# One block of hybrid attention and gated delta rule: the second group's load of the 32x32 inverses goes behind the spill stores on SP's queue

## The chip, the cores and the metric

The kernel runs on one core of one Trainium2 chip. The core has five engines that run side by side: TensorE (PE: matrix products, results in PSUM banks), VectorE (DVE), ScalarE (ACT), GpSimd (POOL) and SyncE (SP). In this kernel all transfers between SBUF and device memory are issued by SP, one after the other, in an order fixed at compile time: an issue that has to wait holds up every issue behind it. The metric is the time of one execution on the device, in microseconds; smaller is better.

## The reference

One transformer block on 1024 tokens of width 1024, in float32. What is computed:

- `h = rmsnorm(x) * (1 + sc1) + sh1`, and `proj = h @ w_in`, which is split into q, k, v of the attention (8 heads of 64) and q, k, v, z, b, a of the gated delta rule (8 heads of 64). `sh1, sc1, g1, sh2, sc2, g2` come from `silu(c) @ w_ada + b_ada`.
- Dilated attention over three window and dilation pairs with a bias by distance, the three results mixed by their softmax denominators.
- The gated delta rule: a causal convolution of width 4 and SiLU on q, k, v; then chunks of tokens, in which a unit lower triangular system is solved,

```python
a_mat = jnp.where(strict, jnp.einsum('nbhcd,nbhed->nbhce', k_beta, kc) * decay, 0.0)
sol = lax.linalg.triangular_solve(a_mat + jnp.eye(CHUNK), rhs, left_side=True, lower=True, unit_diagonal=True)
```

  and a state that is carried from chunk to chunk.
- `x = x + g1 * (concat(attention, delta) @ w_out)`, then a gated feed-forward `(silu(h @ w_gate) * (h @ w_up)) @ w_down`, and a last rmsnorm.

## The kernel before

Every float32 product is done as three products of halves (`hi*hi + lo*hi + hi*lo`): ACT makes the rounded half (`wh`), POOL or DVE the rest (`wl`). Tokens lie in 8 blocks of 128 (`TB`).

**The two groups of delta heads.** `delta(g)` handles four heads at a time: group 0 first, then group 1 (called the second group here). The delta rule is done in chunks of 128, and a chunk's triangular matrix is inverted in two stages in `delta_inverse(g)`. First all 128 diagonal 32x32 blocks of the group (4 heads, 8 chunks, 4 blocks) are inverted at once, one block per partition, by 31 steps of two DVE instructions each (L889, L893). The result `tt` has one inverse in each partition. It is stored to device memory (`tn_d<-tt`, L896) and loaded back as `tn` (L898) with the rows of the blocks on the partitions: 128 partitions of 32 runs of 32 numbers, that is 4096 runs of 128 bytes. Second, four `head`s join the 32x32 inverses to 64x64 and 128x128 by small matmuls (`lv` L921, L937, L941, `lw` L951, `lx` L959), with DVE transposes of `tn` into `U` (L926) and ACT copies of it (L928, L929) beside them. Then `delta_scan(g)` carries the state over the chunks.

**Work counted off ahead.** The projections that are not needed yet are a stream of big matmuls, `others()`, in the order z0, kd, qd, vd, z1 and then, for each pair of attention heads, `va` (L613, eight slices of 24 matmuls, one per token block), the key projection `a4` and the query projection `a0` (L590, two halves of 24 matmuls each). `ahead(us)` takes so many microseconds of that stream by a nominal price (0.64 for three matmuls of 512 columns, 0.32 for three of 256); `until` takes from it until a product is done. `hold(what, us)` does both, and is called once in each `delta_inverse`, at step 0 of the heads: `LEVELS = ("qd", 4), ("z1", 46)`. For the second group z1 is done long before, and by the prices the 46 us are the rest of `va0`, all of `a4_0` and `a0_0`, and six of the eight slices of `va1`. After it, `front` is the last matmul that was counted off and `evicted` the last copy out of PSUM; the heads' first matmuls are put behind `front` on PE, their copies behind `evicted` on ACT. So the heads of the second group begin on PE after the sixth slice of `va1`.

**How a product leaves.** A product is summed up in one of two PSUM banks (`gbank`). ACT copies it, in pieces of 128x256, into a tile with the tag `ev`, of which there are four, and SP stores the tile. `spill` does this for the halves of `kd`, `qd`, `vd`, `a4` and `a0` (copy L1100, store L1101, two of each to a half), `va_evac` for the slices of `va` (copy L1091, store L1092). A tile comes free when its store has landed; a bank when its copies are done. ACT works in order too, so a copy that waits for a tile holds up the copies behind it.

**What sets the order.** The program is traced in Python, and a planner gives each engine a fixed order: it plays the program through with its own estimates of times, and when an engine is free in that play, it takes of the ready instructions the one that was traced first. `urgent()` moves a block 6000 places forward (weight loads L229, the copies out of PSUM; not the stores). `tc.issue_after(x)` adds an edge: what the block traces on the engine of `x` comes behind `x` in that engine's order, with no wait for `x` to end. So the place of a load in SP's queue follows from where it is traced, from when the planner thinks that it is ready, and from such edges.

Of the kernel before, what the change touches and what calls it, by code (L numbers as in the profile page):

```python
# [18 lines left out]
P = 128  # L19
# [4 lines left out]
HALF = 512  # L24
# [7 lines left out]
LEVELS = ("qd", 4), ("z1", 46)  # L32
# [50 lines left out]
def build(tc, I, out):  # L83
    nc = tc.nc
# [20 lines left out]
    def urgent():  # L105
        return tc.high_priority(offset=6000)
# [420 lines left out]
    def scratch(name, n, shape):  # L527
        return [dr.tile(shape, F32, name=f"{name}{i}_d") for i in range(n)]

    class _:  # L530
# [6 lines left out]
        tn = scratch("tn", 2, [P, 1024])  # L537
# [22 lines left out]
    last, taken = [None], [None]  # L560
# [3 lines left out]
    def ahead(us):  # L564

        some = us > 0
        while us > 0:
            w = next(fill[0], None)
            if w is None:
                break  # L570
            us -= w
            used[0] += w
        return some and last[0] is not None
# [296 lines left out]
    def delta_inverse(g, st):  # L870
# [14 lines left out]
        for j in range(31):  # L885
# [9 lines left out]
            )  # L895
        nc.sync.dma_start(_.tn[g], ttf)  # L896
        tn = pr.tile([P, 32, 32], F32, name=f"tn{g}", tag="dt", bufs=2)
        nc.sync.dma_start(  # L898
            tn,
            bass.AP(tensor=_.tn[g].tensor, offset=_.tn[g][0:1, :].offset, ap=[[32, P], [4096, 32], [1, 32]]),  # L900
        )
        st["U"] = []

        def head(hl_):
# [59 lines left out]
        for step in range(3 * SKEW + 8):  # L964
            for h in heads:
                next(h, None)
            if step % SKEW == 0 and step // SKEW < 4:
                if step == 0:
                    hold(*LEVELS[g])
                    front, evicted, quiet[0] = last[0].ins, taken[0], True  # L970
                heads.append(head(step // SKEW))
                with tc.issue_after(front):
                    next(heads[-1])
# [113 lines left out]
    def va_evac(c):  # L1087
# [4 lines left out]
            nc.sync.dma_start(_.va[c][:, :, tb].rearrange("i p d -> p i d"), t.rearrange("p (i d) -> p i d", i=2))  # L1092
        return f

    def spill(name, dst):
        def f(hf, ps):
            for i in range(2):
                t = pv.tile([P, 256], F32, name=f"sp_{name}_{hf}_{i}", tag="ev", bufs=4)
                with urgent():
                    taken[0] = nc.scalar.copy(t, ps[:, 256 * i : 256 * i + 256])  # L1100
                nc.sync.dma_start(dst[:, HALF * hf + 256 * i : HALF * hf + 256 * i + 256], t)  # L1101
        return f

    def va_end(c):
# [46 lines left out]
    def others():  # L1151
        def group1(which):
            for i, (kind, col) in enumerate((("kd", KD), ("qd", QD), ("vd", VD))):
                if kind in which:
                    for q in range(2):
                        yield from proj_d(col + 2 + q, f"{kind}{2 + q}", spill(f"{kind}{q}", _.pj[2 * i + q]))
                    done.add(kind)

        yield from proj_t(I["wz0"], 256, "z0", z_evac(0))
        yield from group1(("kd", "qd", "vd"))  # L1160
        yield from proj_t(I["wz1"], 256, "z1", z_evac(1))
        done.add("z1")
        for hp in range(4):
            if hp < 2:
                yield from proj_t(I["wva"][hp], 256, f"va{hp}", va_end(hp))
                done.add(f"va{hp}")
            for col, kk in ((KA, 4), (QA, 0)):
                yield from proj_d(col + hp, f"a{kk}_{hp}", spill(f"a{kk}_{hp}", _.qk[kk + hp]))
            done.add(hp)
# [11 lines left out]
    quiet = [False]  # L1181
    fill[0] = mixed()

    def hold(what, us):

        until(lambda: what in done)
        ahead(us)

    def until(ready):
        while not ready():  # L1190
            used[0] += next(fill[0])
# [23 lines left out]
    def delta(g, made=(None, None)):  # L1215
        st = {}
        kt = []
        for j in range(4):
            kind, q = ("k", j) if j < 2 else ("q", j - 2)
            hp = 2 * g + q  # L1220
            t = pd.tile([P, T], F32, name=f"{kind}d{hp}", tag=f"{kind}d", bufs=2)
            (kd if kind == "k" else qd)[hp] = t
            if g == 0:
                conv((4 if kind == "k" else 0) + hp, xps[j], t)
                kt.append(delta_turn(g, kind, q, t, norms=norms[0], keep=kind == "k"))
                if j == 1:
                    nc.scalar.activation(norms[0]["lr"], norms[0]["rk"], AF.Ln, bias=eps1)
            else:
                nc.sync.dma_start(t, _.cv[j])
                if kind == "k":  # L1230
                    kt.append(delta_turn(g, kind, q, t, keep=True))
        delta_prep(g, st, norms[g], kt[0:2], made[0] or delta_rows(g))
        if g == 1:
            until(lambda: "vd" in done)
        delta_v(g, st, [lambda q=q: vxp[q] if g == 0 else fetch(4 + q, f"v{2 + q}") for q in range(2)], made[1])
        delta_inverse(g, st)
        until(lambda: ("qd", "z1")[g] in done)
        delta_scan(g, st)
        return None if g else delta_early()
# [289 lines left out]
    for hf in range(2):  # L1529
# [4 lines left out]
        for d in range(KT):  # L1534
            slabs = [(wsplit(I["wo"][d, 0], 512, f"wo{d}_0_{hf}"), 0)]
            t = x2[d, hf]
# [206 lines left out]
    for k in range(4):  # L1743
# [3 lines left out]
        t = px.tile([P, HALF], F32, name=f"t2_{k}", tag="m", bufs=5)  # L1747
# [260 lines left out]
```

## Time and profile before

| | |
|---|---|
| time, median of 3 runs | 1400.84 us (1399.38 to 1406.18) |
| the profiled execution's own time | 1404.82 us |
| its span, first to last instruction | 1403.1 us |
| PE busy, share of the span | 1350.7 us, 96% |
| DVE, ACT, POOL busy | 63%, 47%, 20% |
| mean granted TensorE clock | 0.988 |

The profile has rows of groups of instructions (line, engine, operation, output <- input, count, durations), waits (who stood idle until what), a timeline, and busy times in stretches of the span. `SPq` is the issue of a transfer: its time is that of issuing, not of moving the data. In the timeline, neighbouring instructions of one kind are merged into one row with a count. PEclk is the clock that TensorE was granted, 1.00 at full speed. All positions are microseconds from the start of the span.

### The profile page before, as it was taken

How to read it: one execution, taken by the hardware profiler on the slowest of the kernel's cores; microseconds unless marked ns; L12 is line 12 of the kernel's file. 1: busy time of each engine (PE TensorE's matmuls, PEld its weight loads, DVE VectorE, ACT ScalarE, POOL GpSimd, SP SyncE). 2: the span in 40 equal slices, each digit the busy share in tenths (PEclk: the TensorE clock that was granted, in tenths of full speed). 3: DMA queues.
4: the chain of work that ended last, by engine and by line, in shares of the span. 5: the costliest groups of instructions: out<-in, count | busy, mean ns of one | idle time of the engine just before them, and what ended most of it. 6: DMA issues, size and time to landing. Idle time of an engine off the chain costs nothing.

```text
span 1403.1 us, 24422 instructions
## 1 busy us (share of the span) xinstructions
PE 1350.7 (96%) x8984; PEld 1114.8 (79%) x8984; DVE 877.0 (63%) x1677; ACT 661.7 (47%) x1287; POOL 284.1 (20%) x267
## 2 busy tenths in 40 slices
PE   8999999999989899999999999999999999999998
PEld 4778887888888777778877878888888888888876
DVE  3687484666825433666228987667575776474497
ACT  4497424356224255766147743333333333444455
POOL 2346412344213244443162000000000000000000
PEclk9999899999999999999999999999999999999999
DMA  8665565475452355441584345444453665765575
GB/s 309 224 194 167 138 219 175 135 250 173 129 144 68 104 164 173 141 123 54 180 262 151 121 165 173 165 160 166 139 196 113 210 210 187 257 225 191 191 263 195
DMA packets 169872, 245.68 MB, mean 175 GB/s; under 512 B 32566, under 2 KB 73831, under 8 KB 169752
## 3 DMA queue, kind: packets, MB, share of 16 engines
q1 hardware_dynamic: 169752, 244.12, 53.4%
q8 instruction: 71, 1.16, 0.3%
q14 instruction: 49, 0.40, 0.1%
HBM read 181.30 MB, written 67.48 MB: 177 GB/s over the span
## 4 chain that ended last, share of the span: by engine, by line
PE 54%; DVE 5%; DMA 3%; issue 2%; ACT 2%; POOL 1%; SPq 0%; DVEq 0%; ACTq 0%; POOLq 0%
PE wua L1602 9%; PE wga L1602 8%; PE X L1802 6%; PE wo L590 5%; PE wgc L1602 4%; PE wuc L1602 4%; PE g_a L590 3%; PE Z L1802 3%; PE wgb L1602 2%; PE y L1359 2%; PE Y L1802 2%; PE wub L1602 2%; PE tr L1338 2%; PE S L1314 1%; PE S L1315 1%
## 5 line engine op out<-in xcount | busy, mean ns | idle before, releaser
L1592 DVE TENSOR_TENSOR wl_db<-wr_db,wh_db 128x512 fp32r<-128x512 f32 x77 | 52.9, 690 | 67.0 <-ACT wh_db L1591 66.8
L1591 ACT CAST wh_db<-wr_db 128x512 fp32r<-128x512 f32 x77 | 47.5, 622 | 85.3 <-PE X L1802 39.4
L1318 DVE CUSTOM_DVE_ANT_0 X<-S,ng 128x512 f32<-128x512 f32 (+3 forms) x64 | 36.9, 587 | 60.0 <-PE S L1315 40.0
L1325 POOL TENSOR_SCALAR X<-X,sc 128x128 f32<-128x128 f32 (+7 forms) x64 | 49.0, 769 | 77.1 <-DVE sc L1324 71.6
L1802 PE MATMUL X<-wl_db,wh_da 128*128 128x512 f32 x160 | 62.4, 390 | 0.3 <-DVE wl_db L1592 0.3
L1802 PE MATMUL X<-wh_db,wl_da 128*128 128x512 f32 x160 | 62.3, 389 | 0.0
L1802 PE MATMUL X<-wh_db,wh_da 128*128 128x512 f32 x160 | 62.3, 389 | 0.0
L1323 ACT ACTIVATE X<-X,sc 128x128 f32<-128x128 f32 (+7 forms) x64 | 49.5, 775 | 25.1 <-DVE sc L1318 23.5
L1592 DVE TENSOR_TENSOR wl_da<-wr_da,wh_da 128x512 fp32r<-128x512 f32 x77 | 52.8, 686 | 4.2 <-ACT wh_da L1591 4.2
L1591 ACT CAST wh_da<-wr_da 128x512 fp32r<-128x512 f32 x77 | 47.5, 617 | 16.0 <-DMA wr_da<-ao_d 9.4
L590 PE MATMUL g_a<-hh,wh_a 128*128 128x512 f32 x128 | 52.8, 413 | 0.0
L590 PE MATMUL wo<-yl,wh_wo 128*128 128x512 f32 x128 | 50.6, 396 | 1.9 <-DVE yl L1422 1.9
L590 PE MATMUL wo<-yh,wh_wo 128*128 128x512 f32 x128 | 51.9, 408 | 0.0
L590 PE MATMUL g_a<-hh,wl_a 128*128 128x512 f32 x128 | 51.6, 403 | 0.0
L590 PE MATMUL g_a<-hl,wh_a 128*128 128x512 f32 x128 | 51.6, 403 | 0.0
L1338 PE MATMUL tr<-ident,X 128*128 128x128 f32 x288 | 46.0, 279 | 5.4 <-POOL X L1325 2.6
L590 PE MATMUL wo<-yh,wl_wo 128*128 128x512 f32 x128 | 50.9, 398 | 0.0
L1591 ACT CAST wh_wg_s<-wg_s 128x512 fp32r<-128x512 f32 x33 | 20.5, 623 | 56.1 <-PE wuc L1602 23.8
L1338 PEld LDWEIGHTS tr<-ident,X 128*128 128x128 f32 x288 | 32.8, 140 | 17.7 <-POOL X L1325 6.7
L231 POOL TENSOR_TENSOR wl_wo<-wr_wo,wh_wo 128x512 fp32r<-128x512 f32 x24 | 32.0, 1334 | 59.5 <-ACT wh_wo L230 55.3
L613 PE MATMUL g_va<-wh_va,hh 128*128 128x256 f32 x128 | 38.6, 301 | 3.9 <-ACT va L1091 3.9
L1591 ACT CAST wh_wg<-wr_wg 128x512 fp32r<-128x512 f32 x31 | 19.2, 622 | 46.0 <-PE wua L1602 18.9
(553 smaller groups left out, 4365.0 us busy)
## 6 DMA issues: line engine op xcount, KB each, us to landing
wm<-in_wada SPq DMA_DIRECT2D x44, 512.0 KB, 5.9
wr_da<-ao_d SPq DMA_DIRECT2D x77, 256.0 KB, 3.0
wr_wu<-in_wu SPq DMA_DIRECT2D x50, 256.0 KB, 2.7
wr_wg<-in_wg SPq DMA_DIRECT2D x48, 256.0 KB, 3.0
ao_d<-a SPq DMA_DIRECT2D x44, 256.0 KB, 2.3
wr_wd<-in_wdn SPq DMA_DIRECT2D x44, 256.0 KB, 3.1
wr_db<-wt_d SPq DMA_DIRECT2D x44, 256.0 KB, 2.8
ao_d<-as SPq DMA_DIRECT2D x33, 256.0 KB, 2.0
```

Source lines behind the costliest of these rows:

```text
L231: (eng or nc.gpsimd).tensor_tensor(out=lo[:, :n], in0=raw[:, :n], in1=hi[:, :n].bitcast(F32), op=ALU.subtract)
L590: last[0] = nc.tensor.matmul(ps, a[:, w0], b[k0 + k4][:, cs], start=(i == 0), stop=(i == n - 1))
L613: last[0] = nc.tensor.matmul(ps[:, :n], a[k][:, ts_], b[:, w0], start=(i == 0), stop=(i == 23))
L1318: nc.vector.tensor_tensor_reduce(out=X[:, c0:c1], in0=ps[:, 0 : c1 - c0], in1=ng[:, u + c0 : u + c1], scale=1.0, scalar=(3e38 if m is None ...
L1323: nc.scalar.activation(X[:, 0:nk], X[:, 0:nk], AF.Exp, scale=-1.0, bias=m, accum_out=sc[:, 2:3])
L1325: nc.gpsimd.tensor_scalar(out=X[:, 0:nk], in0=X[:, 0:nk], scalar1=sc[:, 3:4], scalar2=0.0, op0=ALU.mult, op1=ALU.add)
L1338: nc.tensor.transpose(ps[:, (kb - c0) * P : (kb - c0 + 1) * P], X[:, kb * P : kb * P + P], ident)
L1359: ins = nc.tensor.matmul(yps[64 * e : 64 * e + 64, (q % 4) * P : (q % 4 + 1) * P], va[:, kb, 64 * e : 64 * e + 64], ets[q % 2][e][:, kb, : ...
L1591: nc.scalar.copy(hi, src)
L1592: (eng or nc.vector).tensor_tensor(out=lo, in0=src, in1=hi.bitcast(F32), op=ALU.subtract)
L1602: nc.tensor.matmul(ps, a[:, w0], b, start=(first and k == 0 and n_ == 0), stop=(k == 3 and n_ == 2), skip_group_check=True,)
L1802: nc.tensor.matmul(bank[b], a[:, ts_], w, start=(first and n_ == 0), stop=(last and n_ == 2), skip_group_check=True,)
```

## The change

Three edits. The call of `hold` and the line that notes `front` and `evicted` move from step 0 of the heads to a place ahead of the load of `tn`, in both groups; nothing else is traced between the two places except that load. For the second group (`if g`) the load gets an edge behind `spilled[0]`, the last store that `spill` has traced by then. And `spill` keeps that store. By the order of the stream this is the second store of the second half of `a0_0`.

```diff
         nc.sync.dma_start(_.tn[g], ttf)
         tn = pr.tile([P, 32, 32], F32, name=f"tn{g}", tag="dt", bufs=2)
-        nc.sync.dma_start(
-            tn,
-            bass.AP(tensor=_.tn[g].tensor, offset=_.tn[g][0:1, :].offset, ap=[[32, P], [4096, 32], [1, 32]]),
-        )
+        hold(*LEVELS[g])
+        front, evicted, quiet[0] = last[0].ins, taken[0], True
+        with tc.issue_after(spilled[0].ins) if g else ExitStack():
+            nc.sync.dma_start(
+                tn,
+                bass.AP(tensor=_.tn[g].tensor, offset=_.tn[g][0:1, :].offset, ap=[[32, P], [4096, 32], [1, 32]]),
+            )
         st["U"] = []
...
             if step % SKEW == 0 and step // SKEW < 4:
-                if step == 0:
-                    hold(*LEVELS[g])
-                    front, evicted, quiet[0] = last[0].ins, taken[0], True
                 heads.append(head(step // SKEW))
...
+    spilled = [None]
+
     def spill(name, dst):
         def f(hf, ps):
             for i in range(2):
                 t = pv.tile([P, 256], F32, name=f"sp_{name}_{hf}_{i}", tag="ev", bufs=4)
                 with urgent():
                     taken[0] = nc.scalar.copy(t, ps[:, 256 * i : 256 * i + 256])
-                nc.sync.dma_start(dst[:, HALF * hf + 256 * i : HALF * hf + 256 * i + 256], t)
+                spilled[0] = nc.sync.dma_start(dst[:, HALF * hf + 256 * i : HALF * hf + 256 * i + 256], t)
         return f
```

## The prediction

> **What bounds the kernel now.** I read the page first, then PE's waits. PE is busy nearly all the time, so a change is worth what it takes out of PE's few idle places and out of the stretches in which PE is granted less than full clock. One of the longest of these waits lies where the change is.
>
> ```profile
> PE 1350.7 (96%) x8984; PEld 1114.8 (79%) x8984; DVE 877.0 (63%) x1677; ACT 661.7 (47%) x1287; POOL 284.1 (20%) x267
> ...
> PE g_va L613 <- ACT va L1091: 3.9, 1, 3.9
> ...
> ACT va L1091 <- DMA qk_d<-sp_a: 8.9, 2, 8.2
> ```
>
> So PE waited once, 3.9 us, for ACT to copy a slice of `va1` out of PSUM, and ACT had waited 8.2 us for the store of a spilled piece of `a0_0` to land, since the four `ev` tiles were taken. The timeline of SP's queue shows why that store was late (start, duration, line, transfer):
>
> ```profile
> 387.97 0.32 SPq L896 DMA_DIRECT2D tn_d<-tt  x1
> 388.50 1.12 SPq L1275 DMA_DIRECT2D raw<-qk_d  x2
> 390.78 0.38 SPq L898 DMA_DIRECT2D tn<-tn_d  x1
> 391.25 2.58 SPq L229 DMA_DIRECT2D wr_a<-in_wd  x1
> 393.88 0.43 SPq L1101 DMA_DIRECT2D qk_d<-sp_a  x1
> 394.41 0.38 SPq L229 DMA_DIRECT2D wr_a<-in_wd  x1
> 394.83 1.45 SPq L1101 DMA_DIRECT2D qk_d<-sp_a  x3
> 397.36 0.37 SPq L1092 DMA_DIRECT2D va_d<-va  x1
> ```
>
> The last two of the four spills were copied by 388.8 (ACT row below), yet the first is issued at 393.88. Between lie two things that belong to `tn`: SP waits from 389.62 to 390.78 for the store `tn_d` to land, and the issue right behind the load of 4096 short runs takes 2.58 us. That this goes with `tn` and not with the weight load is seen in the durations of both groups: the issue behind the first group's `tn` is a `wm` (207.69) that took 4.07, and both are the longest of their lines (the first two rows: min/median/max in ns):
>
> ```profile
> L229 SPq DMA_DIRECT2D wr_a<-in_wd x16: 328/333/2582, 317.0 to 494.3; - x16
> L1123 SPq DMA_DIRECT2D wm<-in_wada x32: 368/419/4067, 52.3 to 356.2; - x32
> ...
> 207.69 4.07 SPq L1123 DMA_DIRECT2D wm<-in_wada  x1
> ...
> 388.12 0.64 ACT L1100 COPY sp_a<-g_a 128x256 f32<-128x256 f32 x2
> 388.30 1.30 POOL L231 TENSOR_TENSOR wl_a<-wr_a,wh_a 128x512 fp32r<-128x512 f32 x1 [1.43 <-ACT wh_a L230]
> 396.96 0.37 ACT L1091 COPY va<-g_va 128x256 f32<-128x256 f32 x1 [8.20 <-DMA qk_d<-sp_a]
> ```
>
> On PE the wait costs more than its length. Matmuls of `va1` start every 0.12 us up to 393.21; the next starts at 397.39, and then they come slower until 400.67, while the granted clock is half:
>
> ```profile
> 393.09 0.28 PE L613 MATMUL g_va<-wh_va,hl 128*128 128x256 f32 x1
> 393.21 0.28 PE L613 MATMUL g_va<-wl_va,hh 128*128 128x256 f32 x1
> 397.39 0.58 PE L613 MATMUL g_va<-wh_va,hh 128*128 128x256 f32 x1 [3.89 <-ACT va L1091]
> ...
> 400.54 0.29 PE L613 MATMUL g_va<-wl_va,hh 128*128 128x256 f32 x1
> 400.67 0.28 PE L613 MATMUL g_va<-wh_va,hh 128*128 128x256 f32 x1
> ...
> 398.00:399.00 1.00, 1.00 (x6) 1.00 (x6) 0.00 (x0) 0.38 (x1) 0.00 (x0) 0.50 0.47 142
> 399.00:400.00 1.00, 1.00 (x7) 1.00 (x6) 0.00 (x0) 0.00 (x0) 0.00 (x0) 0.50 0.10 37
> ```
>
> Due at 393.33, started at 397.39: 4.06 us. The 15 steps from 397.39 to 400.67 took 3.28 us where 15 x 0.12 = 1.80 would do: 1.48 us by the clock. Together 5.54 us is what this place can give.
>
> **The change part by part.** *The second group's spills come earlier.* With the load of `tn` behind the fourth spill, SP has after the two `raw` loads (389.62) the first `wr_a`. Its tile is free by then: the last split on POOL before it ends at 389.60. So it issues at about 389.7 for 0.33, and the first spill at about 390.1 and not 393.88. From its issue to ACT's copy took 396.96 - 393.88 = 3.08, and from that copy to PE 397.39 - 396.96 = 0.43. PE then goes on at 390.1 + 3.08 + 0.43 = 393.6, against 393.33 due: 0.3 us of wait are left. The landing times of these stores lie between 1.7 and 3.1 us, so the rest is 0 to 0.3:
>
> ```profile
> DMA to landing us min/median/max: 1.7/2.8/3.1
> ```
>
> I take 0.3, since 3.08 is the row of this very store. Gain in waiting: 397.39 - 393.6 = 3.8 us.
>
> *The clock.* An idle time of 0.3 us should leave it at full speed: the first group had 0.83 us in one place and was granted 1.00 in that stretch, whereas about 1.9 us missing between 462 and 466 was followed by half clock.
>
> ```profile
> 218.25 0.50 PE L590 MATMUL g_vd<-hh,wh_vd 128*128 128x512 f32 x1 [0.83 <-ACT sp_qd L1100]
> ...
> 215.00:220.00 5.00, 4.17 (x47) 2.99 (x46) 0.59 (x3) 2.11 (x6) 1.67 (x2) 1.00 1.03 370
> 462.00:464.00 2.00, 0.60 (x3) 0.16 (x1) 1.19 (x1) 0.00 (x0) 2.00 (x2) 1.00 0.00 0
> 464.00:466.00 2.00, 1.46 (x9) 1.27 (x10) 1.53 (x6) 0.32 (x2) 0.01 (x1) 0.85 0.40 134
> 466.00:468.00 2.00, 2.00 (x11) 2.00 (x11) 0.72 (x3) 0.58 (x2) 0.72 (x1) 0.50 0.43 129
> ```
>
> So the 1.48 us go as well, with the ends 0 (if half a wait still lowers the clock) and 1.48. [...]
>
> *The load of `tn` comes later.* The spills and the second `wr_a` take from 390.1 the same 393.88 to 396.28 = 2.4 us that they take in the rows above, so the load goes at about 392.5, or 1.7 us later than now. From issue to use took 395.46 - 390.78 = 4.68 here and 213.17 - 207.22 = 5.95 in the first group:
>
> ```profile
> 395.46 1.78 DVE L926 STREAM_TRANSPOSE U<-tn 32x256 f32<-32x256 f32 x4 [7.52 <-DMA tn<-tn_d]
> 410.48 1.20 PE L921 MATMUL lv<-tn,dt 32*32 32x32 f32 x64
> ...
> 204.32 0.34 SPq L896 DMA_DIRECT2D tn_d<-tt  x1
> ...
> 207.22 0.37 SPq L898 DMA_DIRECT2D tn<-tn_d  x1
> ...
> 213.17 1.79 DVE L926 STREAM_TRANSPOSE U<-tn 32x256 f32<-32x256 f32 x4 [0.79 <-DMA tn<-tn_d]
> 219.14 0.69 PE L921 MATMUL lv<-tn,dt 32*32 32x32 f32 x32
> ```
>
> It is there by 397.2 to 398.5. PE wants it where the counted-off matmuls end, now at 410.48 and then at 410.48 - 5.3 = 405.2. The cover is those matmuls of `va1`, 6.7 to 8 us of it is left, and the transposes (1.78) fit too. Price nothing; if the cover were gone, each us of delay would be one on PE.
>
> *What stands behind the load on SP.* The slow issue, 2.58 to 4.07 us, now falls on whatever is next, probably the store of the first `va1` slice, copied at 393.6. It would be issued by 392.9 + 4.1 = 397 at the latest, and land some 3 us later, at 400. The tile that it frees is wanted by the fifth slice, the third that PE makes after 393.6, so done and copied at 393.6 + 3 x 24 x 0.12 = 402.2. Price nothing. The `raw` loads behind it feed the attention, far later.
>
> *The first group.* `hold` is traced ahead of its load too, with no edge. The load loses its precedence over the stores of what is counted off, nothing else. When it is ready in the planner's play, it can only be overtaken by a store that is ready at that moment. I take no change of order, hence 0; the ends are -0.8 (the 0.83 us above goes, if stores step ahead and tiles come free sooner) and the second rival's price.
>
> *Downstream.* After the heads PE is tied to data that its own earlier work makes, and weight loads to tiles that it frees, so a shift should last to the end.
>
> **Sum:** -3.8 - 1.5 = -5.3 us. The profiled execution would be 1404.82 - 5.3 = 1399.5 us (span 1397.8). It lies 4.0 us above the median of the runs; nothing in the trace says that the place differs in them, so I set the same 5.3 us against the median: 1395.5 us.
>
> **The rivals.** *First: the wait comes back elsewhere or stays.* For it: ACT is in order and four tiles are few, so another late store on SP (a `raw` load that waits, a slower landing beside two 256 KB loads) can hold the same copy. Against it: nothing else in the rows stands between 389.62 and the spill. If 2 us of wait and the clock loss are left, the gain is 4.06 - 2.0 = 2.1 us, 1398.7 us; if all comes back, 1400.8.
>
> *Second, the slower side: the first group's load falls back.* Its store of `tn_d` goes at 204.32, and spills of `qd` follow at 212.32 (three) and 219.73 (two):
>
> ```profile
> 212.32 1.47 SPq L1101 DMA_DIRECT2D pj_d<-sp_qd  x3
> ...
> 219.73 1.73 SPq L1101 DMA_DIRECT2D pj_d<-sp_qd  x2
> ```
>
> Behind the first three the load goes at 213.8, is there at 213.8 + 5.95 = 219.8, and PE waits 0.6 us at 219.14. Behind the last two it goes at 221.5, is there at 227.4, and PE waits 8.3 us and loses about 1.5 by the clock: 1395.5 + 9.8 = 1405.3 us. It costs PE something from an issue at 219.14 - 5.95 = 213.2 on, and outweighs the gain from about 217 on. Against it: now it goes at 207.22, before those copies are made, and no edge holds it.
>
> *Third: a spell of half clock more or less.* The one after 465 costs by the windows 0.15 x 2 at 464 to 466, 0.5 x 6 from 466 to 472 and 0.06 x 2 after, some 3.4 us; the waits before it are short, so with all of it 5.3 us earlier it may not come: 1395.5 - 3.4 = 1392.1 us. [...]
>
> ```profile
> 470.00:472.00 2.00, 2.00 (x8) 1.81 (x8) 0.53 (x3) 0.37 (x1) 0.61 (x1) 0.50 0.00 0
> 472.00:474.00 2.00, 2.00 (x17) 1.84 (x17) 0.85 (x4) 0.88 (x3) 0.97 (x1) 0.94 0.23 70
> ```
>
> **How the numbers follow.** The sum as worked out 0.58, with 1393 to 1399 as its own range; the first rival 0.16; the second, or another order by the planner of like price, 0.16; the third 0.10. A range of 1391 to 1405 us leaves out the dearer half of the second and a little of the others, under 2 in 10. Faster or slower by over 0.5% (7.0 us, about what a measurement of this kernel can tell from no change) means under 1393.8 or over 1407.8. Faster: most of the third and a fifth of the first case, 0.20. Slower: the dear end of the second, 0.12. Within: 0.68. So I expect a real gain that is smaller than this bound.
>
> **What would show it.** Right: the four spills ahead of the `tn` load on SP, the first at about 390; a long issue behind `tn`; PE's wait for `va` under 0.5 us, with clock 1.00 from 393 on; `lv` of the second group at about 405 with no wait for `tn`. Wrong: a wait for `tn` at `lv` in either group, an `ev` wait of the old length, or a different order of PE's matmuls. The prediction falls if the planner, having the load at another place, orders other queues anew.

## The result, and the profile after

The changed kernel takes 1399.68 us (median of 20 executions, 1393.02 to 1404.38), the kernel before 1404.66 us beside it (20 executions, 1398.2 to 1407.79). The ratio is 0.9965, with a 95% interval of 0.9949 to 0.9981: 0.35% faster, 4.98 us by the medians, less than the 0.5% named in the prediction. The profiled execution took 1400.45 us with a span of 1398.7, against 1404.82 and 1403.1 before.

First the page of the changed kernel:

```profile
PE 1345.5 (96%) x8984; PEld 1110.1 (79%) x8984; DVE 877.8 (63%) x1677; ACT 661.6 (47%) x1287; POOL 284.7 (20%) x267
```

PE is busy 5.2 us less for the same 8984 matmuls; the mean granted clock was 0.991, against 0.988 before. The place of the change in the timeline (start, duration, engine, line, transfer or operation; SP's queue first, then ACT, PE and DVE):

```profile
386.45 0.32 SPq L896 DMA_DIRECT2D tn_d<-tt  x1
386.99 1.12 SPq L1277 DMA_DIRECT2D raw<-qk_d  x2
388.16 1.06 SPq L1103 DMA_DIRECT2D qk_d<-sp_a  x2
389.27 0.43 SPq L229 DMA_DIRECT2D wr_a<-in_wd  x1
389.80 0.40 SPq L1103 DMA_DIRECT2D qk_d<-sp_a  x1
390.24 0.44 SPq L229 DMA_DIRECT2D wr_a<-in_wd  x1
390.78 0.44 SPq L1103 DMA_DIRECT2D qk_d<-sp_a  x1
391.27 0.44 SPq L901 DMA_DIRECT2D tn<-tn_d  x1
392.58 3.17 SPq L1092 DMA_DIRECT2D va_d<-va  x2
...
387.12 0.64 ACT L1102 COPY sp_a<-g_a 128x256 f32<-128x256 f32 x2
392.19 0.76 ACT L1091 COPY va<-g_va 128x256 f32<-128x256 f32 x2 [4.42 <-DMA qk_d<-sp_a]
...
392.21 0.28 PE L613 MATMUL g_va<-wl_va,hh 128*128 128x256 f32 x1
392.61 0.39 PE L613 MATMUL g_va<-wh_va,hh 128*128 128x256 f32 x1
...
396.61 1.79 DVE L929 STREAM_TRANSPOSE U<-tn 32x256 f32<-32x256 f32 x4 [10.19 <-DMA tn<-tn_d]
404.32 1.20 PE L924 MATMUL lv<-tn,dt 32*32 32x32 f32 x64
```

All four spills stand ahead of the load. PE starts its next matmul 0.40 us after the last one before it, where 0.12 is the step in full flow and where it was 397.39 - 393.21 = 4.18 before. The clock stays whole (the stretch, its length, then busy time of PE, weight loads, DVE, ACT, POOL, then the granted clock, DMA share and GB/s):

```profile
388.00:404.00 16.00, 15.88 (x133) 15.68 (x132) 1.75 (x4) 3.83 (x11) 0.59 (x1) 1.00 1.05 270
```

What this place gave can be read from three points that both traces have. The copies of the last two spilled pieces stand at 388.12 before and 387.12 after: the changed kernel's execution was already 1.00 us ahead, by work that has nothing to do with this place. The first matmul behind the wait stands at 397.39 and 392.61: 4.78 ahead. The first `lv` of the heads stands at 410.48 and 404.32: 6.16 ahead. So the place gave 3.78 us of waiting and 1.38 us by the clock, 5.16 us together.

The two executions differ elsewhere too, so that the span is 4.4 us shorter and not 6.2. At the attention's first `S` the lead has grown to 8.60 us, since this execution has no half clock near 465 (its clock is 1.00 in the stretch from 460 to 475; the row before, then after):

```profile
483.09 0.33 PE L1314 MATMUL S<-KS,QS 128*128 128x128 f32 x1 [1.15 <-ACT yt L1072]
474.49 0.33 PE L1316 MATMUL S<-KS,QS 128*128 128x128 f32 x1 [0.97 <-ACT yt L1072]
```

Near 540 it shrinks by almost 5 us. In the stretch from 507 to 545 DVE waited longer for the attention's bias `ng` (`us in total, times, longest`; 1.7 us, once, in the same part of the profile before), PE waited 2.06 and 2.72 us close behind it, and the clock was 0.51 in the stretch from 536 to 543:

```profile
DVE X L1320 <- DMA ng<-Rb_d: 5.3, 2, 3.0
```

In two more profiles of the same kernel, below, this wait was 0.7 and 3.3 us in the same part. It differs from execution to execution, and nothing shows it to be a price of the change: over the whole span DVE waited 11.8 us for `ng` in the profile before and 6.8 us here.

In the first group one thing moved after all:

```profile
205.12 0.39 SPq L1103 DMA_DIRECT2D pj_d<-sp_qd  x1
205.60 0.38 SPq L901 DMA_DIRECT2D tn<-tn_d  x1
206.08 4.69 SPq L1125 DMA_DIRECT2D wm<-in_wada  x2
```

One store of `qd` now goes ahead of the load of `tn`, and PE's wait of 0.83 us for a copy of `qd` is gone from this trace. The orders of PE, ACT, DVE and POOL are those of the kernel before; only SP's queue is another.

### The profile page after: what moved, and what is told of

Its sections match the earlier page's. It is cut to its first block, busy times and chain, and to the rows that moved or that the text cites. A ratio compares the mean times of both kernels' runs of the same rounds, so it can differ in the third digit from the quotient of the medians.

```text
span 1398.7 us, 24417 instructions
## 1 busy us (share of the span) xinstructions
PE 1345.5 (96%) x8984; PEld 1110.1 (79%) x8984; DVE 877.8 (63%) x1677; ACT 661.6 (47%) x1287; POOL 284.7 (20%) x267
## 3 DMA queue, kind: packets, MB, share of 16 engines
q8 instruction: 71, 1.16, 0.3%
## 4 chain that ended last, share of the span: by engine, by line
PE 54%; DVE 5%; DMA 3%; issue 2%; ACT 1%; POOL 1%; SPq 0%; DVEq 0%; ACTq 0%; POOLq 0%
PE wua L1604 9%; PE wga L1604 8%; PE X L1804 6%; PE wgc L1604 4%; PE wuc L1604 4%; PE wo L590 4%; PE g_a L590 3%; PE Z L1804 3%; PE wgb L1604 2%; PE Y L1804 2%; PE wub L1604 2%; PE y L1361 2%; PE tr L1340 2%; PE S L1316 1%; DMA ng<-Rb_d 1%
## 5 line engine op out<-in xcount | busy, mean ns | idle before, releaser
L1593 ACT CAST wh_wu_s<-wu_s 128x512 fp32r<-128x512 f32 x33 | 20.4, 621 | 44.0 <-PE wga L1604 17.2
```

What stands on the lines that cost most here:

```text
L1593: nc.scalar.copy(hi, src)
```

## The experiments

The theory after the result: the whole gain comes from the second group, where the first copies of `va1` find their tiles free about 4 us sooner; the first group gives little; the load itself has some 7 us of cover. The rivals: the first group's step gives a part; the load's issue, not its place ahead of the spills, is the cost; what is left of the wait is noise, or hangs on something that can be removed.

### The changed kernel again

No edit.

> The changed kernel once more, for a second profile of it. Theory A (the gain is made in SP's queue, in the second group): PE's wait for ACT's copy of va1 stays under 0.3 us, the lead over the profile of before grows by about 5.1 us between 388 and 401 us, as in the first profile (from 1.0 to 6.2), and the time is 4 to 6 us under before. The other differences between the two first profiles (2 us before 200, 1.8 us at 466 to 472, minus 5 us at 535 to 546) come out otherwise here if they are chance of one execution (spells of half clock, landing times), and the same if they belong to the change: then the attention waits 2 to 3 us each for two loads of ng again.

Measured: 1399.25 us, ratio 0.9962 (0.9941 to 0.9982). The time is the same, but a wait under 0.3 us, as expected, did not come: this execution's profile shows the place in another state. Timeline:

```profile
386.03 0.64 ACT L1102 COPY sp_a<-g_a 128x256 f32<-128x256 f32 x2
387.80 0.32 SPq L896 DMA_DIRECT2D tn_d<-tt  x1
389.51 1.05 SPq L1103 DMA_DIRECT2D qk_d<-sp_a  x2
393.31 0.81 ACT L1091 COPY va<-g_va 128x256 f32<-128x256 f32 x2 [6.63 <-DMA qk_d<-sp_a]
393.73 0.39 PE L613 MATMUL g_va<-wh_va,hh 128*128 128x256 f32 x1 [2.33 <-ACT va L1091]
```

PE waits 2.33 us, though SP's order is the same. The store `tn_d` needs DVE to have made the inverses, and it stands ahead of the spills in SP's queue. Against the copies of the last spilled pieces it is issued 386.45 - 387.12 = -0.67 us in the first profile and 387.80 - 386.03 = +1.77 us here: 2.44 us later, and PE waits 2.2 us more. What made DVE late is in the groups of its operations between 320 and 390 (busy, mean ns, then idle before, and for what), first the changed kernel's first profile, then this one:

```profile
L889 DVE TENSOR_TENSOR tm<-nt,tt 128x31 f32<-128x31 f32 (+15 forms) x31 | 13.4, 434 | 1.0
L878 DVE TENSOR_TENSOR nt<-nt,bpr 128x1024 f32<-128x1024 f32 x1 | 1.2, 1225 | 4.2 <-DMA nt<-lt_d 4.2
```

```profile
L889 DVE TENSOR_TENSOR tm<-nt,tt 128x31 f32<-128x31 f32 (+15 forms) x31 | 14.7, 475 | 1.0
L878 DVE TENSOR_TENSOR nt<-nt,bpr 128x1024 f32<-128x1024 f32 x1 | 1.2, 1224 | 5.4 <-DMA nt<-lt_d 5.4
```

The load of `nt`, at the start of the inverses, was waited for 1.2 us longer, and the 31 products took 1.3 us longer: 2.5 us. Over all profiles of kernels with this order of SP's queue, and of the two that shift only the load, the waits are these:

| profile | `tn_d` issued, against the last copies of `a0_0` | PE's wait for the copy of `va` |
|---|---|---|
| the changed kernel, first | -0.67 | 0.1 |
| the same with the loads of `ng` in halves (below) | -0.46 | 0.1 |
| second group alone | -0.45 | 0.2 |
| the changed kernel, third | -0.44 | 0.1 |
| load behind the third store of `va1` | -0.70 | 0.1 |
| load behind the first two spills | +0.20 | 0.9 |
| the changed kernel, again | +1.77 | 2.3 |

Up to about -0.4 the wait is hidden. Beyond it lie two profiles only, one of them with the load at another place; by these two, every us by which DVE ends later against PE is roughly one us of wait. The kernel before had -0.15 at this place, just past the bend, where a line between the rows -0.44 and +0.20 gives some 0.5 us.

And the clock (stretches of this profile):

```profile
395.00:396.00 1.00, 1.00 (x7) 1.00 (x6) 0.00 (x0) 0.00 (x0) 0.00 (x0) 0.50 1.28 236
...
398.00:400.00 2.00, 2.00 (x20) 2.00 (x19) 0.78 (x2) 0.37 (x1) 0.00 (x0) 1.00 0.54 146
```

The wait of 2.33 us is followed by half clock (0.73 in the stretch from 394 to 395, 0.50 from 395 to 397, 0.56 from 397 to 398), as the wait of 4.06 us was in the kernel before, and it costs as much: from the first matmul behind the wait to the first `lv` (406.92 here) it is 406.92 - 393.73 = 13.19 us, against 13.09 before and 11.71 in the first profile. Against the profile before, this execution is 2.09 us ahead at the last copies and 3.56 at the first `lv`. So here the place gave 1.5 us and not 5.

### The second group alone

```diff
-        hold(*LEVELS[g])
-        front, evicted, quiet[0] = last[0].ins, taken[0], True
+        if g == 1:
+            hold(*LEVELS[g])
+            front, evicted, quiet[0] = last[0].ins, taken[0], True
...
+                if step == 0 and g == 0:
+                    hold(*LEVELS[g])
+                    front, evicted, quiet[0] = last[0].ins, taken[0], True
```

> The change in the second group alone; the first group's load of tn stays ahead of hold, as before. Theory A: the six issues that move in SP's queue are the whole of it, so 4.5 to 5.5 us under before, PE's wait for va1 gone, and the 0.8 us wait of the first group (vd, for ACT's copy of qd) still there. Rival B (the first group's store that steps ahead of its load of tn gives a good part): under 3 us.

Measured: 1398.33 us, ratio 0.9962 (0.9937 to 0.9988), the whole gain. Its waits of PE:

```profile
PE g_vd L590 <- ACT sp_qd L1106: 1.2, 1, 1.2
```

The first group's wait is there and the second group's is 0.2 us. The gain is the second group's, as far as the interval tells.

### The first group alone

```diff
-        hold(*LEVELS[g])
-        front, evicted, quiet[0] = last[0].ins, taken[0], True
-        with tc.issue_after(spilled[0].ins) if g else ExitStack():
+        if g == 0:
+            hold(*LEVELS[g])
+            front, evicted, quiet[0] = last[0].ins, taken[0], True
+        with ExitStack():
...
+                if step == 0 and g == 1:
+                    hold(*LEVELS[g])
+                    front, evicted, quiet[0] = last[0].ins, taken[0], True
```

> The change in the first group alone: one store of qd steps ahead of the load of tn there; the second group as before. Theory A: 0.8 us or less under before, not to be told from none; in the profile the wait of PE for ACT's copy of qd (0.83 us) is gone and the wait of 3.9 us at va1 with the half clock behind it is there. Rival B: 2 us or more under before.

Measured: 1402.3 us, ratio 0.9987 (0.9963 to 1.0011). The first group's wait is gone and the second group's is back, 3.3 us, with a clock of 0.89 behind it:

```profile
388.00:404.00 16.00, 12.71 (x94) 12.51 (x93) 1.74 (x4) 2.71 (x8) 0.00 (x0) 0.89 0.85 217
```

The step in the first group may be worth the 0.8 to 1.2 us that its wait takes; the interval does not tell that from nothing.

### The load later still: behind the third store of `va1`

```diff
-        with tc.issue_after(spilled[0].ins) if g else ExitStack():
+        with tc.issue_after(stored[-3].ins) if g else ExitStack():
...
-            nc.sync.dma_start(_.va[c][:, :, tb].rearrange("i p d -> p i d"), t.rearrange("p (i d) -> p i d", i=2))
+            stored.append(nc.sync.dma_start(_.va[c][:, :, tb].rearrange("i p d -> p i d"), t.rearrange("p (i d) -> p i d", i=2)))
```

> As the changed kernel, but the second group's load of tn goes behind the store of the third slice of va1 (all other engines keep their order), about 6 us later: issued at about 397, there by 402 to 403. Theory A with the cover as I worked it out (the load is wanted when the counted-off matmuls end, at about 404 to 405): no wait of PE for it, the same time as the changed kernel within 1 us, that is 4 to 6 us under before. Rival C (the cover is thinner, for the heads' copies and transposes need tn earlier than lv does): PE waits 1 to 3 us at the heads, and half or all of the gain is lost.

Measured: 1400.7 us, ratio 0.9972 (0.9945 to 1.0). Timeline and PE's waits:

```profile
400.30 0.48 SPq L901 DMA_DIRECT2D tn<-tn_d  x1
407.00 1.79 DVE L929 STREAM_TRANSPOSE U<-tn 32x256 f32<-32x256 f32 x4 [17.53 <-DMA tn<-tn_d]
...
PE lv L940 <- DVE cs L936: 0.3, 1, 0.3
```

The load goes at 400.30 and not at the 397 expected. Against the last copies of `a0_0` (390.20 here) that is 5.95 us later than in the changed kernel, and the heads begin without a wait for it: 0.3 us behind the first step is all. That is where the cover ends, at some 6 us of later issue, since the load took 6.70 us from issue to use here and 5.34 in the changed kernel. The estimate of 6.7 to 8 us is about right: in the changed kernel `lv` starts 404.32 - 396.61 = 7.71 us after the load is there.

### The load by long runs

The kernel before with one edit: the second group's inverses are read as 128 runs of 4 KB in place of 4096 runs of 128 bytes. The numbers then lie in another layout, so this kernel serves for its times alone.

```diff
-            tn,
-            bass.AP(tensor=_.tn[g].tensor, offset=_.tn[g][0:1, :].offset, ap=[[32, P], [4096, 32], [1, 32]]),
+            tn if g == 0 else tn.rearrange("p a b -> p (a b)"),
+            bass.AP(tensor=_.tn[g].tensor, offset=_.tn[g][0:1, :].offset, ap=[[32, P], [4096, 32], [1, 32]])
+            if g == 0 else _.tn[g],
```

> The kernel before, with the second group's inverses read from the same place as 128 runs of 4 KB and not as 4096 runs of 128 bytes (the numbers then lie in another layout, so the delta rule's output of those four heads is not the reference's; every other part is as it was). Theory: the many short runs make the issue behind this load slow. Then the weight load behind it issues in 0.33 to 0.45 us and not in 2.58, the first spill goes 2.2 us earlier against PE than in the kernel before, PE's wait for the copy of va falls from 4.06 to about 1.8 us, and the time by 2 to 3.5 us, ratio 0.9975 to 0.9985. Rival: whatever stands behind the load is held, since SP has just waited for the store of the inverses to land; then the issue stays at 2.5 us or more, the wait at about 3.9 us, and the ratio is 1.000.

Measured: 1405.58 us, ratio 1.001 (0.9988 to 1.0033), and in the profile PE waited 2.76 us, where about 1.8 was expected. This profile cannot be laid beside the others as a whole, since it has a long stretch of half clock in the first group, told of in the last section. So it was run once more:

> The second group's inverses as 128 runs of 4 KB once more, since the profile of the first such run had a long stretch of half clock behind the first group's wait (the delta rule's output of four heads is not the reference's, as before). Theory: the issue behind the load is 0.33 to 0.45 us again, and the first spill takes 5 us and not 3 from its issue to the copy, as in the first run, so that PE's wait is 2.5 to 3 us and the time falls by no more than 1 to 2 us: ratio 0.9985 to 0.9995. Rival: the 5 us were chance; then the wait is about 1 us or less, and the ratio 0.997.

Measured: 1401.64 us, ratio 0.9984 (0.9963 to 1.0005). Timeline of the second run, and its waits:

```profile
391.47 0.33 SPq L898 DMA_DIRECT2D tn<-tn_d  x1
391.90 0.38 SPq L1102 DMA_DIRECT2D qk_d<-sp_a  x1
392.32 0.43 SPq L229 DMA_DIRECT2D wr_a<-in_wd  x1
396.58 0.37 ACT L1092 COPY va<-g_va 128x256 f32<-128x256 f32 x1 [6.57 <-DMA qk_d<-sp_a]
...
PE g_va L613 <- ACT va L1092: 2.3, 1, 2.3
```

The issue behind the load is a short one now, 0.38 us. It is also another one, since the planner puts the first spill there and not a weight load; but behind the short runs stores are slow to issue as well (4.65 us for two stores of `va1` in the second profile of the changed kernel). So the short runs do make that issue slow. But the spill is no longer the quick transfer of before: from its issue to ACT's copy it takes 4.68 us (5.17 in the first run), where it took 3.08. Counted from the issue of the load, ACT's copy comes after 396.58 - 391.47 = 5.11 us and 414.78 - 409.18 = 5.60 us, against 396.96 - 390.78 = 6.18 us in the kernel before. Of the delay that the load puts on the spills behind it, the slow issue, with the weight load that stood between, is 0.6 to 1.1 us; the rest stays when the runs are long, and goes only when the spills stand ahead. That the rest is the time in which the load's 512 KB and the spills are moved side by side is an estimate from the rows (DVE first reads the load at 396.15, 4.68 us after its issue as in the kernel before, and ACT's copy starts 0.4 us behind that); it was not isolated.

### The load behind the first two spills

```diff
-        with tc.issue_after(spilled[0].ins) if g else ExitStack():
+        with tc.issue_after(spilled[-4].ins) if g else ExitStack():
...
-    spilled = [None]
+    spilled = []
...
-                spilled[0] = nc.sync.dma_start(dst[:, HALF * hf + 256 * i : HALF * hf + 256 * i + 256], t)
+                spilled.append(nc.sync.dma_start(dst[:, HALF * hf + 256 * i : HALF * hf + 256 * i + 256], t))
```

> The changed kernel with the second group's load behind the first two of the four spills only; the two others and the two weight loads stand behind it. Theory: PE's wait comes from the first copies of va, which want the tiles of the first two spills; then PE's wait there is as in the changed kernel (0.1 to 2.3 us), the slow issue (2.6 to 4.7 us) falls on a weight load, the last two spills go at about 393.5 and free their tiles at 397.5, some 1.7 us after the third slice is done, which the second PSUM bank covers but for 0 to 0.5 us: ratio 0.9955 to 0.9975. Rival: the slow issue still stands ahead of two of the four tiles, so the wait comes back one or two slices later: PE waits 1.5 us or more there, half clock behind it, and the ratio is 0.998 to 1.000.

Measured: 1398.28 us, ratio 0.996 (0.9942 to 0.9979). Timeline and stretch:

```profile
388.96 0.43 SPq L901 DMA_DIRECT2D tn<-tn_d  x1
389.49 3.78 SPq L229 DMA_DIRECT2D wr_a<-in_wd  x2
393.32 0.90 SPq L1103 DMA_DIRECT2D qk_d<-sp_a  x2
396.57 0.37 ACT L1091 COPY va<-g_va 128x256 f32<-128x256 f32 x1 [4.13 <-DMA qk_d<-sp_a]
...
388.00:404.00 16.00, 15.10 (x128) 14.77 (x128) 1.74 (x4) 4.08 (x11) 0.00 (x0) 1.00 0.96 233
```

The slow issue falls on the weight loads, the last two spills go 4.4 us after the load, and the third copy of `va1` has to wait for them. PE does not: 0.9 us is lost before the first copies, as the table above has it for +0.20, and none later. So only the first two tiles need to come free early here. That the second PSUM bank covers the others is the likely reason.

### The store of the inverses behind the first two spills

The table says that what is left of the wait hangs on the store `tn_d`. SP stands idle for it until DVE is done, while two `raw` loads and two spills behind it are ready. This edit traces `hold` ahead of that store and puts the store behind the first two spills:

```diff
-        nc.sync.dma_start(_.tn[g], ttf)
-        tn = pr.tile([P, 32, 32], F32, name=f"tn{g}", tag="dt", bufs=2)
         hold(*LEVELS[g])
         front, evicted, quiet[0] = last[0].ins, taken[0], True
-        with tc.issue_after(spilled[0].ins) if g else ExitStack():
+        with tc.issue_after(spilled[-3].ins) if g else ExitStack():
+            nc.sync.dma_start(_.tn[g], ttf)
+        tn = pr.tile([P, 32, 32], F32, name=f"tn{g}", tag="dt", bufs=2)
+        with tc.issue_after(spilled[-1].ins) if g else ExitStack():
...
```

> The changed kernel with one step more: in the second group the store of the inverses, which makes SP stand from 378.8 to 386.45 until DVE has made them, goes behind the first two spills, which ACT has copied by 382. Orders of the other engines are those of the changed kernel. Theory: what is left of PE's wait (0.1 to 2.3 us by the execution) hangs on when DVE ends against PE, since two raw loads and two spills stand behind that store; with the two spills at about 382 the first copies of va find free tiles whatever DVE does, PE's wait is 0.2 us or less with clock 1.00 from 388 to 404, and the time is 0.5 to 2 us below the changed kernel, ratio 0.995 to 0.9965. Rival: the wait hangs on the last two spills too, which still stand behind the store of the inverses; then 1 us or more of it stays in an execution in which DVE ends late, and the ratio is that of the changed kernel, 0.996 to 0.997.

Measured: 1398.57 us, ratio 0.9952 (0.993 to 0.9974). One of its seven executions took 4912 us; nothing shows why, and the ratio leaves it out. Timeline and stretch:

```profile
380.94 1.12 SPq L1278 DMA_DIRECT2D raw<-qk_d  x2
382.11 1.05 SPq L1104 DMA_DIRECT2D qk_d<-sp_a  x2
386.50 0.32 SPq L899 DMA_DIRECT2D tn_d<-tt  x1
389.25 0.37 ACT L1092 COPY va<-g_va 128x256 f32<-128x256 f32 x1 [1.93 <-issue]
...
388.00:404.00 16.00, 16.00 (x162) 15.87 (x162) 1.74 (x4) 4.54 (x12) 0.14 (x1) 1.00 0.91 228
```

The two spills go at 382.11, ACT's copy no longer waits for a store, and PE is busy 16.00 of 16.00 us. Then the same once more, with the changed kernel beside it on one chip:

> The kernel with the store of the inverses behind the first two spills, once more, beside the changed kernel on the same chip. Theory: the time that PE stands at the copies of va is 0 in every execution of it, and 0.1 to 2.3 us in those of the changed kernel, so it is 0.3 to 1 us faster in the median: ratio 0.995 to 0.9965 here against 0.9957 to 0.997 for the changed kernel. Rival: the two are the same, and 0.9952 was chance.

> The changed kernel as it is, for the comparison with the one above: ratio 0.9957 to 0.997. Its wait for the copy of va lies between 0.1 us (SP's store of the inverses early against PE) and 2.3 us (late); every us by which that store goes later against PE adds one to the wait.

Measured: 1394.55 us, ratio 0.9928 (0.9901 to 0.9955), for the edit; 1397.09 us, 0.9949 (0.9927 to 0.9971), for the changed kernel. PE was again busy 16.00 of 16.00 in the edit's profile. Beside the changed kernel on one chip it has the lower time, by 2.5 us, but the intervals overlap, and its first ratio, 0.9952, lies among those of the changed kernel (0.9949 to 0.9965). That it takes the wait away in two profiles is shown; whether it is faster than the changed kernel is not settled. In its two profiles `tn_d` was issued 0.17 and 0.16 us ahead of the last copies (386.50 against 386.67, 385.69 against 385.85). Between the rows -0.44 and +0.20 of the table that would be a wait of some 0.4 to 0.5 us, and there was none. An execution with DVE as late as +1.77 was not seen.

### The loads of `ng` in halves

```diff
-            nc.sync.dma_start(
-                ng[e],
-                bass.AP(tensor=_.R.tensor, offset=_.R[2 * hp + e, 0:1, :].offset + 127, ap=[[1151, P], [1, T]]),
-            )
+            for c in (HALF, 0):
+                nc.sync.dma_start(
+                    ng[e][:, c : c + HALF],
+                    bass.AP(tensor=_.R.tensor, offset=_.R[2 * hp + e, 0:1, :].offset + 127 + c, ap=[[1151, P], [1, HALF]]),
+                )
```

> The changed kernel with each load of the attention's distance bias ng issued as two halves by columns, the later columns first. Theory: the wait of DVE for the first ng (0.7 to 5.3 us in the profiles so far, with no change in the order of issues) is the landing time of one load of 512 KB; by halves the part that is wanted first is there sooner, the wait falls to 1 us or less, and the time by 1 to 3 us against the changed kernel, ratio 0.994 to 0.996 against the kernel before. Rival: the same bytes move through the same engines beside the same other loads, and the wait stays where it is; ratio 0.996 to 0.997.

Measured: 1400.13 us, ratio 0.997 (0.9952 to 0.9987). In the same part as above DVE waited 3.0 us in all for `ng`, 2.4 at the longest: the wait stays, and the rival holds. Halving the load does not bring it sooner. Why the same loads land so differently from one execution to the next stays open.

## Why the prediction was right, and where not

**The size.** The forecast was 5.3 us less than before, 3.8 of waiting and 1.5 by the clock. The place gave 3.78 and 1.38 in the profiled execution, and the medians differ by 4.98. That these agree so well is in part luck, since another execution of the same kernel had 1.5 us at this place, and the executions differ by several us elsewhere. The absolute time, 1395.5, came out 4.2 us low at 1399.68, within the whole range and 0.7 us above the 1393 to 1399 that the sum had as its own, and the step that failed is the choice of the base: "so I set the same 5.3 us against the median". The three executions shown had a median of 1400.84; with twenty it is 1404.66, and 1404.19, 1403.74 and 1404.57 in the other comparisons. The profiled execution (1404.82), 4.0 us above the shown median, was the better base, by chance near the median of twenty: its own forecast, 1399.5, is within 0.2 us of the result.

**What held the spills.** The prediction put it down to SP's wait for `tn_d` (1.16 us) and the slow issue (2.58). The order is right and the slow issue is real, but the step "from its issue to ACT's copy took 3.08" took that time to be the spill's own, whatever stands ahead of it. It is not: it was 4.03 in the changed kernel, and 4.68 and 5.17 where the load's issue was short. The forecast for the wait left, 0.3 us, came out (0.28 by the starts of the matmuls, 0.1 as the profile counts it) because two errors cancelled: the spills were issued 388.16 - 387.12 = 1.04 us after the last copies and not 390.1 - 388.12 = 1.98, and they took 0.95 us longer to be through. Of the 0.94 us by which they went sooner, 0.42 is theirs, as two of them go ahead of the weight load; 0.52 is this execution's, in which `tn_d` was issued at -0.67 against the copies and not at -0.15.

**"0 to 0.3 us are left".** That holds when DVE ends early against PE. It was too narrow a span: one of the profiles of the changed kernel has 2.33. This is the first rival's figure (2 us of wait and the clock loss left), to which the prediction gave a cause of another kind, a late `raw` load or slow landing. The cause is the store `tn_d`, which it had taken as a fixed point in time.

**The clock.** The 1.48 us went, as 1.38. The end of 0, "if half a wait still lowers the clock", has its cases in the runs: waits a little over half as long as the 4.06 us of before were followed by half clock, 2.33 us in the second profile of the changed kernel (0.73 from 394 to 395, 0.50 from 395 to 397) and 2.26 us in the second run with long runs (0.58 from 398 to 399, 0.50 from 399 to 401). The wait of 0.9 us with the load behind the first two spills left the clock at 1.00 from 388 to 404. So in these runs the loss by the clock went where the wait was down to 0.1 or 0.9 us, and not where it was 2.3.

**The load of `tn`.** Issue at about 392.5, there by 397.2 to 398.5, `lv` at about 405: measured 391.27, 396.61 and 404.32, with no wait. The cover of 6.7 to 8 us is 7.71 in these rows, and the load behind the third store of `va1`, with 5.95 us of it used, found hardly any left.

**The slow issue falls on a store of `va1`, at no price.** Right: 3.17 us for two stores, and no wait behind it.

**The first group.** "I take no change of order, hence 0" failed; its end of -0.8 came true. One store stepped ahead of the load and the wait of 0.83 us went. In the time it cannot be told from nothing (0.9987, 0.9963 to 1.0011). The second rival, the load falling far back, did not come: it went at 205.60, well before 213.2.

**The third rival.** The stretch of half clock near 465 was absent from the changed kernel's first profile and present in its second (clock 1.00 and 0.77 in the stretch from 460 to 475). Its price is less than the 3.4 us of the prediction: from 6.16 at the first `lv` to 8.60 at the first `S` the lead grew by 2.4 us. Whether the change makes it rarer is open: in the same stretch the clock was 0.77 in the kernel before, in the second group alone and in the first group alone, and 0.89 with the load behind the third store of `va1`. The wait of 1.9 us ahead of it (`st` for DVE's `R`) ends at 464.54 in the profile before, with a clock of 0.50 from 466 to 472, and at 458.39 in the changed kernel's first profile, with a clock of 1.00 from 452 to 470.

## What to carry to other kernels

In a queue that is served in order, look at the wait of the store that frees a tile and not only at the wait of the tile's user: a load that PE wanted only 15 us after it was there (395.46 and 410.48) put a wait of 4 us on the busiest engine by standing ahead of such a store. Put first what others wait for, and check that the moved load still has cover. Next, look at what still stands ahead of it: here it is a store that depends on an engine not tied to the one that waits, so the rest of the wait varies between executions, and a single profile shows it at 0.1 or 2.3 us. And take the base of an absolute forecast from as many executions as there are: three of them missed the median of twenty by 3.8 us, almost the size of the effect.

## What was not expected of the hardware

**Short waits and long stretches at half clock.** In the first run with long runs PE waited 1.82 us in the first group. Stretches of that profile, then the same of the changed kernel:

```profile
216.00:218.00 2.00, 0.26 (x2) 0.00 (x0) 0.00 (x0) 0.34 (x2) 0.00 (x0) 1.00 1.09 406
218.00:220.00 2.00, 1.91 (x27) 1.22 (x29) 0.47 (x2) 1.92 (x7) 0.00 (x0) 0.62 1.03 404
220.00:252.00 32.00, 32.00 (x331) 23.09 (x328) 7.42 (x16) 8.35 (x21) 5.05 (x6) 0.50 0.29 91
```

```profile
220.00:252.00 32.00, 32.00 (x485) 24.61 (x484) 16.22 (x33) 12.42 (x28) 8.70 (x11) 1.00 0.46 143
```

PE was busy in all of these 32 us behind the wait and yet stayed at half clock (0.50 against 1.00); it did 331 instructions where the changed kernel's execution did 485. The page of that profile has the granted clock at 5 and 7 tenths in the two of its slices from 213 to 284 us, so that the half clock lasted, by an estimate from these digits, until somewhere from 263 to 270, some 45 to 51 us in all. That execution took 1423.4 us, the longest of its ten. A wait of 1.2 us at the same place, in the run of the second group alone, did nothing of the kind: the clock was 1.00 from 210 to 226. Against that, 1.9 us at another place (PE's `trv` for ACT's `vd`, near 148), in the third profile of the changed kernel, left the clock at 1.00 from 146 to 154. So a wait near 2 us is a risk that a mean does not show: here it was followed by nothing (1.9 us), by less than full clock from 394 to 398 (2.33 us), or by some 45 to 51 us of it (1.82 us). What kept the clock down so long with PE busy stays open.

**An issue behind many short runs.** In the rows shown, the issue behind a load of 4096 runs of 128 bytes took 2.58 and 4.07 us where it stands alone, and 3.17 to 4.69 with the issue that follows it in the same row; behind the same 512 KB in 128 runs it took 0.38.
